# Where in the queues the transfers stand that form sums of the output weights in DRAM

## The chip, the cores and the metric

The kernel runs on one core of one Trainium2 chip. The metric is device time in microseconds (us), lower is better. The kernel before was timed three times; the median is 1558.39 us. One further execution was recorded by the hardware profiler, and all rows quoted below are from it.

Engine names are those of the profile: PE is the matrix engine, PEld its weight loads, DVE the vector engine, ACT the scalar engine, POOL the GpSimd engine. SP only issues transfers (DMAs). A "q" behind an engine's name means its instruction queue, which issues DMAs. DMA queue q1 holds what SP issues, q0 what POOL issues, q10 what ACT issues.

## What is computed

One encoder layer on a sequence of 1024 tokens with model width 1024, in float32. Cut to what matters here:

```python
h = rmsnorm(x, g_mix)
z = h @ w_in                    # pooling channels | q | k | v, 8 heads
y_pool = pool_mixer(z[:, :512], ...)
y_attn = diff_attention(q, k, v, ...)          # two softmax maps per head
gates = sigmoid(h @ w_gate + b_gate)           # 2 x 1024 columns
merged = gates[:, :1024] * (y_pool @ w_branch_pool) \
       + gates[:, 1024:] * (y_attn @ w_branch_attn)
x = x + merged @ w_out
x = x + square(relu(rmsnorm(x, g_ffn) @ w_up)) @ w_down
```

The product with `w_out` is made with seven block products in place of eight. For that it needs sums of the 512 x 512 quarters of `w_out`; with the quarters 11, 12, 21, 22, they are T1 = 11 + 12, T3 = 22 + 12, T2 = 22 + 12 + 11 and T4 = 22 + 12 + 11 + 21 (the signs are handled elsewhere).

## The kernel before, in words

Every float32 product runs as three matmuls on halves of the operands. A helper `split` (lines 132 and 133) makes the halves: ACT writes the high one, and DVE or POOL subtracts to get the low one. `mm3` (lines 139 to 141) issues the three matmuls.

**Startup.** SP loads `x` in eight tiles of 128 tokens, the weights of head 0 in four pairs (`rqkv`, each pair two DMAs of 192 KB) and small vectors. PE runs warm-up products with no use (`warm`), then, for each tile of tokens, transposes the normed tile `hn` into `hT` (lines 564 and 289). The early instructions pass through a helper `q` (line 439), which keeps the written order on each engine. The tiles 0 to 3 of `x` come first; the tiles 4 to 7 are loaded by line 437, outside that fixed order.

**Heads.** A loop of token steps `g` (line 932) covers 8 heads of 8 tiles, 64 steps in all. In each step a written order of stages (`ORDER`) takes the projection `z` (stage A), its normalization (stage B, line 273 on POOL in `rsq`, one step later), the transposes of q and k (C), the scores (D) and so on. Stage W, two steps ahead of a head, loads the next head's weights (`load_w`) and has them split with POOL (`split_w`, lines 132 and 133). Between the steps, fill work is dealt out two steps to a unit: columns of the gate product (`gate_cols`, tiles `frgate`, `fwgate`, `g`) and the pooling groups. A gate column is two units; its weights are loaded by `fill_w` (line 314) in two DMAs of 256 KB and split with POOL.

**The order that is written is not the order that runs.** A planner takes each instruction in order of its place in the program as soon as its inputs and its engine are free by the planner's own clock. Work without inputs is thus issued far ahead of the step in which it is written. `tc.issue_after(ins)` adds one rule: what stands in its block, as far as it is on the engine of `ins`, is issued behind `ins` in that engine's queue. It is an order of issue, with no wait for `ins` to finish.

**The sums.** `sum_steps` (line 919) forms T1 to T4 in DRAM. Four plain copies of 1 MB, issued by SP (line 924), write one quarter into each sum. Seven accumulating DMAs of 1 MB, issued by POOL (line 927), add the others; an add waits for the transfer that wrote the same sum before. The generator is advanced from the token loop (lines 954 and 955): at step 12 all four copies, then one add at each of the steps 18, 24, 30, 36, 42, 48 and 54. Nothing else orders them. After the heads, `w_set` (line 1085) loads the sums with the other operands of the output product (tile `ro`); the first such load of a sum is issued at 848.0 us.

**After the heads** come the two branch products, the gating, the output product (seven products on the sums), the second norm, and the two products of the feed-forward part.

Of the kernel before, what the change touches and what calls it, by code (L numbers as in the profile page):

```python
# [12 lines left out]
ALU = mybir.AluOpType  # L13
# [30 lines left out]
N_W1, N_W2 = 9, 16  # L44
POOL_W = (3,)
G_DIST, G_COLS = 3, 2
SUM_FROM, SUM_STEP = 12, 6

O = "B1 C2 H7 D4 R8 E5 F6 W-2 A0"
ORDER = [(w[0], int(w[1:])) for w in O.split()]  # L50
# [14 lines left out]
def encoder_kernel(  # L65
# [21 lines left out]
    nc = tc.nc  # L87
# [42 lines left out]
    def split(hi, lo, src, lo_eng=None):  # L130

        made = nc.scalar.copy(hi, src)  # L132
        (lo_eng or nc.vector).tensor_tensor(lo, src, f(hi), op=ALU.subtract)  # L133
        return made
# [20 lines left out]
    def fw_tile(shape, name, dt=F32R):  # L155
        return fwpool.tile(shape, dt, tag="fw", name=name)
# [4 lines left out]
    def fr_tile(shape, name):  # L161
        return fp.tile(shape, F32, tag="fr", name=name, bufs=N_FR)
# [90 lines left out]
    mhalf = const.tile([P, NT], F32, name="mhalf")  # L253
# [13 lines left out]
    yd = dram.tile([S, D], F32, name="yd")  # L267
    w_sum = [dram.tile([S // 2, D], F32, name=f"w_sum{i}") for i in range(2)]

    def rsq(dst, ss, n, c):  # L270

        nc.vector.tensor_scalar(dst, ss, c, EPS, op0=ALU.mult, op1=ALU.add)  # L272
        nc.gpsimd.tensor_tensor(dst, dst, mhalf[:, :n], op=ALU.pow)  # L273

    def norm_transpose(xt, gb, t, dst, hn, small, banks):

        th, c0 = t // 4, (t % 4) * P
        ss = small.tile([P, 1], F32, tag="ss", name=f"ss{t}", bufs=2)
        rs = small.tile([P, 1], F32, tag="rs", name=f"rs{t}", bufs=2)
        nc.scalar.activation(hn, xt, AF.Square, accum_out=ss)  # L280
        rsq(rs, ss, 1, 1.0 / D)
        for j in range(2):
            js = slice(j * 512, (j + 1) * 512)
            nc.vector.scalar_tensor_tensor(hn[:, js], xt[:, js], rs, gb[:, js], op0=ALU.mult, op1=ALU.mult)
            trp, trtag = banks[j % len(banks)]
            ps = trp.tile([P, 512], F32, tag=trtag, name=f"hps{t}_{j}")
            for i in range(4):
                k = 4 * j + i
                nc.tensor.transpose(ps[:, i * P : (i + 1) * P], hn[:, k * P : (k + 1) * P], identf)
            for i in range(2):  # L290
                kp = 2 * j + i
                src = ps[:, i * 256 : (i + 1) * 256].rearrange("p (a b) -> p a b", a=2)
                h_hi[t] = split(dst[kp, th, 0][:, :, c0 : c0 + P], dst[kp, th, 1][:, :, c0 : c0 + P], src)
# [16 lines left out]
    def fill_w(src, c0, name):  # L310
        ws = []
        for j in range(2):
            rw = fr_tile([P, 4, P], f"fr{name}_{j}")
            nc.sync.dma_start(
                rw, src[j * 512 : (j + 1) * 512, c0 : c0 + P].rearrange("(kk p) c -> p kk c", p=P)
            )
            w = fw_tile([P, 2, 4, P], f"fw{name}_{j}")
            split(w[:, 0], w[:, 1], rw, nc.gpsimd)
            ws.append(w)
        return ws  # L320
# [22 lines left out]
    def pool_group(g):  # L343
        win = WINDOWS[g]
        ws = fill_w(w_in, g * P, f"pool{g}")
        rg = fr_tile([P, P], f"rgrp{g}")
        nc.sync.dma_start(rg, w_pool_grp[g])
# [35 lines left out]
    def gate_cols(c):  # L383
        with first_gates(c) if c < 3 else nullcontext():
            ws = fill_w(w_gate, c * P, f"gate{c}")
        for th in range(2):
            ps = fill_proj(ws, th, f"g{c}_{th}", spare_bank if c >= G_Z else fill_bank)
            fo = fo_tile(f"go{c}_{th}")
            nc.scalar.activation(fo[:, 0:512], ps, AF.Identity, bias=cols[:, c : c + 1])  # L389
            nc.scalar.dma_start(g_dram[c * P : (c + 1) * P, th * 512 : (th + 1) * 512], fo[:, 0:512])  # L390
            yield
# [23 lines left out]
    with ExitStack() as ph:  # L415
# [279 lines left out]
        def stage_prep(h, t):  # L695
            th = t // 4
            V, ggh = KV[h][1], gghs[h]
            z = st[h, t]["z"]
            sq = s1([P, 256], F32, f"sq{h}_{t}", "sq")
            ms = sp.tile([P, 4], F32, tag="ms", name=f"ms{h}_{t}", bufs=3)  # L700
            nc.scalar.activation(sq, z[:, 0:256], AF.Square)
            nc.vector.tensor_reduce(ms, sq.rearrange("p (a b) -> p a b", a=4), axis=AX.X, op=ALU.add)
            rsq(ms, ms, 4, 1.0 / HD)
            split(V[th][:, t % 4, 0, :], V[th][:, t % 4, 1, :], z[:, 256:384])
            qn = s1([P, 4, HD], F32, f"qn{h}_{t}", "qn", N_QN)
            nc.vector.tensor_tensor(
                qn,
                z[:, 0:256].rearrange("p (a b) -> p a b", a=4),
                ms.unsqueeze(2).broadcast_to([P, 4, HD]),
                op=ALU.mult,  # L710
            )
            nc.gpsimd.tensor_tensor(
                qn[:, 2:4, :], qn[:, 2:4, :], ggh.unsqueeze(1).broadcast_to([P, 2, HD]), op=ALU.mult
            )
            st[h, t] = {"qn": qn}
            yield
# [202 lines left out]
        def sum_steps():  # L919

            q = {f"{i + 1}{j + 1}": w_out[i * 512 : (i + 1) * 512, j * 512 : (j + 1) * 512] for i in range(2) for j in range(2)}
            s = {f"T{i}": w_sum[n][:, c : c + 512] for i, n, c in ((1, 0, 0), (3, 0, 512), (2, 1, 512), (4, 1, 0))}
            for dst, src in (("T1", "11"), ("T3", "22"), ("T2", "22"), ("T4", "22")):
                nc.sync.dma_start(s[dst], q[src])
            yield
            for dst, src in (("T1", "12"), ("T3", "12"), ("T2", "12"), ("T4", "12"), ("T2", "11"), ("T4", "11"), ("T4", "21")):
                nc.gpsimd.dma_start(s[dst], q[src], accum_op=ALU.add)
                yield

        units, made = fillers(), 0  # L930
        sums = sum_steps()
        for g in range(-2, N + 10):
            for t in range(4, NT):
# [186 lines left out]
    def norm_scale(t, src):  # L1120

        ss = squares.pop(t)
        rs = const.tile([P, 1], F32, tag="nrs", name=f"nrs{t}", bufs=2)
        yn = y[t]
        nc.vector.tensor_scalar(rs, ss[:, 0:1], ss[:, 1:2], 1.0 / D, op0=ALU.add, op1=ALU.mult)
        rsq(rs, rs, 1, 1.0)
        for j in range(2):
            js = slice(j * 512, (j + 1) * 512)
            if t < 4:
                nc.vector.scalar_tensor_tensor(yn[:, js], src[j], rs, gfb[:, js], op0=ALU.mult, op1=ALU.mult)  # L1130
            else:
                scaled[t] = nc.vector.tensor_scalar(yn[:, js], src[j], rs, None, op0=ALU.mult)
# [488 lines left out]
```

## Time and profile before

| What | us |
|---|---|
| median of three runs | 1558.39 |
| the three runs | 1558.51, 1558.39, 1557.36 |
| the profiled execution, its own time | 1557.51 |
| span in its trace, first to last instruction | 1555.7 |
| PE busy in the span | 1527.8 |
| DVE, ACT, POOL busy in the span | 1015.3, 794.8, 371.5 |

The span is 1.8 us shorter than the execution's own time, which has a start and an end around it. PE is busy in 98% of the span, but this share counts matmuls at full and at half clock alike. The profile's slices therefore have to be read with the row of the granted clock (PEclk, in tenths) beside the row of PE. A "DMA share" near 1 means that the 16 DMA engines were busy all the time; the GB/s beside it say how much they moved in that time, and the two need not go together.

### The profile page before, as it was taken

The page shows a single profiled execution, that of the slowest core. Times are in us where ns is not written, and L with a number is a line of the kernel's source. Part 1 is how long each engine was busy: PE and PEld are TensorE (multiplying, and loading weights), DVE is VectorE, ACT ScalarE, POOL GpSimd, SP SyncE. Part 2 cuts the span into 40 slices and gives each one's busy share as a digit, 9 for nine tenths or more (in the row PEclk, how much of TensorE's full clock was granted, in tenths as well). Part 3 has the DMA queues.
Part 4 walks back from the last instruction along what each step waited for, and adds up shares of the span by engine and source line. Part 5 has one row for each costly group of instructions (what it writes and reads, how often), then busy time and mean ns, then how long its engine had stood idle before and what let it go on. Part 6 is the DMA issues. An engine that isn't in the chain of part 4 may idle for free.

```text
span 1555.7 us, 21699 instructions
## 1 busy us (share of the span) xinstructions
PE 1527.8 (98%) x7637; PEld 1325.1 (85%) x7637; DVE 1015.3 (65%) x2135; ACT 794.8 (51%) x1653; POOL 371.5 (24%) x457
## 2 busy tenths in 40 slices
PE   7799999999999999999999999999999999999999
PEld 6699999999999999988888887888888878888887
DVE  4477766777677777753444799776665578646662
ACT  4365655555655555554642458565555544333331
POOL 2452515243435343313355530000000000000000
PEclk8799999999999999999999999999999999999999
DMA  9951212111212121326642832546442789637650
GB/s 253 206 125 35 76 36 78 36 55 39 72 40 72 39 76 48 109 78 226 198 158 95 280 146 95 183 154 195 152 143 108 250 313 362 224 122 251 228 191 27
DMA packets 172087, 216.89 MB, mean 139 GB/s; under 512 B 10085, under 2 KB 104010, under 8 KB 171978
## 3 DMA queue, kind: packets, MB, share of 16 engines
q1 hardware_dynamic: 150858, 180.86, 35.3%
q10 hardware_dynamic: 17424, 27.31, 4.8%
q0 software_dynamic: 3696, 7.34, 2.8%
q8 instruction: 60, 0.98, 0.3%
q14 instruction: 49, 0.40, 0.1%
HBM read 161.96 MB, written 65.04 MB: 146 GB/s over the span
## 4 chain that ended last, share of the span: by engine, by line
PE 89%; DMA 5%; DVE 4%; POOL 1%; issue 1%; ACT 1%; POOLq 0%; SPq 0%; ACTq 0%; DVEq 0%
PE z L139 5%; PE z L140 5%; PE z L141 5%; PE Da L140 4%; PE Da L141 4%; PE Da L139 4%; PE g L141 4%; PE g L140 4%; PE g L139 4%; PE Db L139 3%; PE Db L140 3%; PE Db L141 3%; PE X L139 3%; PE X L141 3%; PE X L140 3%; PE sc L769 2%
## 5 line engine op out<-in xcount | busy, mean ns | idle before, releaser
L139 PE MATMUL z<-wqkv,hT 128*128 128x384 f32 x512 | 177.8, 347 | 9.1 <-ACT hT L132 5.8
L141 PE MATMUL z<-wqkv,hT 128*128 128x384 f32 x512 | 176.6, 345 | 0.1
L140 PE MATMUL z<-wqkv,hT 128*128 128x384 f32 x512 | 176.0, 344 | 0.0
L780 ACT ACTIVATE s<-s,nm 128x256 f32<-128x256 f32 (+7 forms) x128 | 99.6, 778 | 78.4 <-DVE nm L772 75.6
L273 POOL TENSOR_TENSOR ms<-ms,mhalf 128x4 f32<-128x4 f32 x64 | 67.4, 1052 | 198.5 <-DVE ms L272 189.1
L139 PEld LDWEIGHTS z<-wqkv,hT 128*128 128x128 f32 x512 | 98.6, 192 | 13.2 <-ACT hT L132 6.8
L139 PE MATMUL g<-hT,fwgate 128*128 128x512 f32 x256 | 100.8, 394 | 0.0
L141 PE MATMUL g<-hT,fwgate 128*128 128x512 f32 x256 | 100.4, 393 | 0.0
L140 PEld LDWEIGHTS z<-wqkv,hT 128*128 128x128 f32 x512 | 98.6, 193 | 2.1 <-DVE wqkv L439 0.3
L140 PE MATMUL g<-hT,fwgate 128*128 128x512 f32 x256 | 100.4, 392 | 0.0
L141 PEld LDWEIGHTS z<-wqkv,hT 128*128 128x128 f32 x512 | 98.3, 192 | 2.0 <-DVE hT L437 0.6
L772 DVE CUSTOM_DVE_ANT_0 s<-sc,dist 128x512 f32<-128x512 f32 (+3 forms) x128 | 74.3, 585 | 20.6 <-PE sc L770 19.7
L769 PE MATMUL sc<-K,Q 128*128 128x512 f32 (+2 forms) x192 | 67.2, 356 | 0.4 <-DVE nm L772 0.4
L770 PE MATMUL sc<-K,Q 128*128 128x512 f32 (+2 forms) x192 | 66.1, 349 | 0.0
L133 DVE TENSOR_TENSOR AS<-s,AS 128x512 fp32r<-128x512 f32 x64 | 43.4, 687 | 33.1 <-ACT AS L132 33.0
L133 POOL TENSOR_TENSOR wqkv<-rqkv,wqkv 128x384 fp32r<-128x384 f32 x56 | 58.8, 1066 | 15.3 <-ACT wqkv L132 12.2
L133 POOL TENSOR_TENSOR fwgate<-frgate,fwgate 128x512 fp32r<-128x512 f32 x32 | 42.4, 1326 | 64.7 <-ACT fwgate L132 62.1
L141 PEld LDWEIGHTS g<-hT,fwgate 128*128 128x128 f32 x256 | 48.1, 188 | 9.5
L139 PEld LDWEIGHTS g<-hT,fwgate 128*128 128x128 f32 x256 | 48.1, 188 | 9.0 <-ACT go L389 0.2
L140 PEld LDWEIGHTS g<-hT,fwgate 128*128 128x128 f32 x256 | 48.1, 188 | 8.8
L133 DVE TENSOR_TENSOR AT_0l<-ta,AT_0h 128x512 fp32r<-128x512 f32 (+1 forms) x48 | 31.9, 665 | 29.4 <-ACT AT_0h L132 29.3
L140 PE MATMUL ba<-yT,wba 128*128 128x512 f32 x128 | 49.8, 389 | 0.0
(483 smaller groups left out, 4603.8 us busy)
## 6 DMA issues: line engine op xcount, KB each, us to landing
wd<-in_w_down_dram SPq DMA_DIRECT2D x56, 512.0 KB, 5.1
wu<-in_w_up_dram SPq DMA_DIRECT2D x32, 512.0 KB, 4.4
udS<-us SPq DMA_DIRECT2D x64, 256.0 KB, 3.0
ur<-udS SPq DMA_DIRECT2D x32, 512.0 KB, 4.8
rqkv<-in_w_in_dram SPq DMA_DIRECT2D x64, 192.0 KB, 2.6
ur<-ud SPq DMA_DIRECT2D x24, 512.0 KB, 5.3
frgate<-in_w_gate_dram SPq DMA_DIRECT2D x32, 256.0 KB, 2.9
g_dram<-go ACTq DMA_DIRECT2D x32, 256.0 KB, 2.1
```

What stands on the lines that cost most here:

```text
L133: (lo_eng or nc.vector).tensor_tensor(lo, src, f(hi), op=ALU.subtract)
L139: nc.tensor.matmul(ps, lhs_hi, rhs_hi, start=first, stop=False, **kw)
L140: nc.tensor.matmul(ps, lhs_hi, rhs_lo, start=False, stop=False, **kw)
L141: return nc.tensor.matmul(ps, lhs_lo, rhs_hi, start=False, stop=last, **kw)
L273: nc.gpsimd.tensor_tensor(dst, dst, mhalf[:, :n], op=ALU.pow)
L769: nc.tensor.matmul(dst, Q[:, i, 0, :], rhs, start=True, stop=False)
L770: nc.tensor.matmul(dst, Q[:, i, 1, :], rhs, start=False, stop=True)
L772: nc.vector.tensor_tensor_reduce(out=s[i][:, c : c + w], in0=sc[:, 0:w], in1=dist[:, o0 + c : o0 + c + w], scale=2.0 ** -(h + 1), scalar=B ...
L780: nc.scalar.activation(s[i][:, 0:n], s[i][:, 0:n], AF.Exp, bias=last, scale=-1.0, accum_out=Z[:, i, t : t + 1])
```

## The change

The transfers of `sum_steps` get a place in their engines' queues, and are dealt out one at a time. Two marks are kept: the last `rsq` instruction on POOL, and the last weight load of the fill work on SP. Each copy is queued behind the latest such load on SP, each add behind the latest `rsq` on POOL. The generator now stops after each copy, and is advanced at every step from 10 on whose number is a multiple of four: the copies at 12, 16, 20 and 24, the adds at 28, 32, 36, 40, 44, 48 and 52. What is moved and added is the same.

```diff
-SUM_FROM, SUM_STEP = 12, 6
+SUM_FROM, SUM_STEP = 10, 4
...
+    marks = {}
+
     def rsq(dst, ss, n, c):
 
         nc.vector.tensor_scalar(dst, ss, c, EPS, op0=ALU.mult, op1=ALU.add)
-        nc.gpsimd.tensor_tensor(dst, dst, mhalf[:, :n], op=ALU.pow)
+        marks["POOL"] = nc.gpsimd.tensor_tensor(dst, dst, mhalf[:, :n], op=ALU.pow).ins
...
-            nc.sync.dma_start(
+            marks["SP"] = nc.sync.dma_start(
                 rw, src[j * 512 : (j + 1) * 512, c0 : c0 + P].rearrange("(kk p) c -> p kk c", p=P)
-            )
+            ).ins
...
             for dst, src in (("T1", "11"), ("T3", "22"), ("T2", "22"), ("T4", "22")):
-                nc.sync.dma_start(s[dst], q[src])
-            yield
+                with tc.issue_after(marks["SP"]):
+                    nc.sync.dma_start(s[dst], q[src])
+                yield
             for dst, src in (("T1", "12"), ("T3", "12"), ("T2", "12"), ("T4", "12"), ("T2", "11"), ("T4", "11"), ("T4", "21")):
-                nc.gpsimd.dma_start(s[dst], q[src], accum_op=ALU.add)
+                with tc.issue_after(marks["POOL"]):
+                    nc.gpsimd.dma_start(s[dst], q[src], accum_op=ALU.add)
                 yield
```

## The prediction

> **What bounds the kernel now.** I read the page's slices first, to find where the matrix engine is not at its peak.
>
> ```profile
> span 1555.7 us, 21699 instructions
> PE   7799999999999999999999999999999999999999
> ...
> PEclk8799999999999999999999999999999999999999
> DMA  9951212111212121326642832546442789637650
> GB/s 253 206 125 35 76 36 78 36 55 39 72 40 72 39 76 48 109 78 226 198 158 95 280 146 95 183 154 195 152 143 108 250 313 362 224 122 251 228 191 27
> ```
>
> Each slice is 38.9 us. The first two show PE idle, the clock below full and the DMA engines full. After that PE is at nine tenths or more to the end. So I cut the first two slices into stages, with the heads as a measure of an undisturbed PE.
>
> ```profile
> core 0: us, PE busy (x) PEld busy (x) DVE busy (x) ACT busy (x) POOL busy (x), PEclk, DMA share, GB/s
> 0.00:10.00 10.00, 6.12 (x36) 5.67 (x36) 0.17 (x1) 1.56 (x2) 2.15 (x26) 1.00 0.76 238
> ...
> 50.00:60.00 10.00, 5.13 (x22) 4.08 (x22) 6.14 (x15) 5.45 (x11) 3.96 (x6) 0.66 1.12 219
> 60.00:70.00 10.00, 4.92 (x15) 3.82 (x16) 3.30 (x10) 3.62 (x9) 3.62 (x4) 0.63 0.56 111
> ...
> 13.20:80.00 66.80, 52.87 (x242) 46.15 (x243) 34.23 (x92) 29.54 (x76) 25.86 (x31) 0.78 0.95 226
> 100.00:600.00 500.00, 500.00 (x2921) 464.29 (x2920) 359.32 (x1093) 287.30 (x742) 195.96 (x268) 1.00 0.18 55
> ```
>
> In the heads, from 100 to 600 us, PE makes 2921 matmuls in 500 us, 0.171 us each, with no idle time. From 13.2 to 80 us it makes 242, worth 242 x 0.171 = 41.4 us, in 66.8 us. So 25.4 us are lost there, part as idle time, part at half clock. The three idle times of PE that matter, and the useless warm-up before them:
>
> ```profile
> 4.15 1.21 PE L439 MATMUL gb<-identf,g_cols 128*128 128x128 f32 x8
> 5.12 2.15 PE L439 MATMUL warm<-ones 128*128 128x256 f32 x16
> 13.23 1.97 PE L439 MATMUL hps<-identf,hn 128*128 128x128 f32 x8 [5.97 <-ACT hn L439]
> ...
> 22.00 0.69 PE L139 MATMUL z<-wqkv,hT 128*128 128x384 f32 x1 [2.76 <-ACT wqkv L439]
> ...
> 64.66 0.69 PE L139 MATMUL z<-wqkv,hT 128*128 128x384 f32 x1 [5.41 <-ACT hT L132]
> ```
>
> Each is traced to a load through the ACT instruction that it waits for:
>
> ```profile
> 9.72 0.63 ACT L439 ACTIVATE hn<-x 128x512 f32<-128x512 f32 x1 [7.08 <-DMA x<-in_x_dram]
> ...
> 21.43 0.51 ACT L439 CAST wqkv<-rqkv 128x384 fp32r<-128x384 f32 x1 [4.29 <-DMA rqkv<-in_w_in_dram]
> ...
> 47.72 1.06 ACT L280 ACTIVATE hn<-x 128x1024 f32<-128x1024 f32 x1 [5.88 <-DMA x<-in_x_dram]
> ...
> 63.72 0.62 ACT L132 CAST fwgate<-frgate 128x512 fp32r<-128x512 f32 x1 [5.17 <-DMA frgate<-in_w_gate_dram]
> ```
>
> The sums are written for steps 12 to 54, but the queues show them in just this stretch, the first copy ahead of everything:
>
> ```profile
> 0.75 0.62 SPq L924 DMA_DIRECT2D w_sum<-in_w_out_dram  x1
> 1.42 1.07 SPq L439 DMA_DIRECT2D x<-in_x_dram  x2
> ...
> 9.71 2.20 SPq L439 DMA_DIRECT2D rqkv<-in_w_in_dram  x4
> ...
> 28.60 2.55 SPq L924 DMA_DIRECT2D w_sum<-in_w_out_dram  x2
> 31.19 5.34 SPq L437 DMA_DIRECT2D x<-in_x_dram  x4
> 40.42 50.79 SPq L314 DMA_DIRECT2D frgate<-in_w_gate_dram  x6
> ```
>
> ```profile
> 9.42 1.29 POOL L927 DMA_DIRECT2D w_sum<-in_w_out_dram  x1 [7.27 <-DMA w_sum<-in_w_out_dram]
> ```
>
> ```profile
> L927 POOL DMA_DIRECT2D w_sum<-in_w_out_dram x7: 1007/1091/1414, 9.4 to 86.7; - x7
> L924 SPq DMA_DIRECT2D w_sum<-in_w_out_dram x4: 507/728/1670, 0.7 to 29.5; - x4
> ...
>   POOL w_sum L927: 19.5, 4
> ...
> DMA to landing us min/median/max: 3.6/12.4/21.3
> ```
>
> All eleven transfers are issued between 0.7 and 86.7 us, 11 MB of what the full DMA engines carry. The weights of head 0 show the effect: the last four of their DMAs go out between 9.71 and 11.91 us, the first add just ahead of them at 9.42 us, and ACT waits for one until 21.43 us. What such loads take by their median over the program:
>
> ```profile
> rqkv<-in_w_in_dram SPq DMA_DIRECT2D x64, 192.0 KB, 2.6
> ...
> frgate<-in_w_gate_dram SPq DMA_DIRECT2D x32, 256.0 KB, 2.9
> ```
>
> **What goes: the first wait.** The first copy leaves the head of SP's queue, so `x` is issued at 0.75 us. By the nearest row, 256 KB in 2.9 us, its first half is there at 3.7 us and the second half, one issue later, by about 4.5. It now starts ACT at 9.72, and from there to the transposes at 13.23 the chain takes 3.5 us. That would give 7.2 to 8.0. Two things hold it back: the gain `gb` ends at 5.36 and must be copied between, and the warm-ups end at 7.27. I take 8.0 us, a gain of 5.2. The bounds are 2.3, if `x` takes twice the row's 2.9 us, and 6.0, when the warm-ups end.
>
> **What goes: the rest of the startup.** With no copy ahead and no add beside them, I let loads land as the medians say. From the transposes on, what is late next is ACT and DVE, which make the operands. I count three remainders of the 25.4 us. Token 0: the casts still come one by one on ACT, 0.5 us each by the row at 21.43, with ACT's other work between them, and PE at full clock needs 3 x 0.17 = 0.5 us for each; I leave 2 us. The three tiles after it have a chain each (norm, transposes, split) that PE cannot run ahead of; another 2 us, an estimate between nothing and the idle time of one such chain. For the tiles 4 to 7, DVE sets the pace:
>
> ```profile
> 50.00:100.00 50.00, 39.87 (x200) 35.50 (x201) 29.66 (x86) 25.91 (x71) 21.85 (x28) 0.83 0.84 163
> ```
>
> DVE is busy 29.66 us here, and PE has 200 x 0.171 = 34.2 us worth of matmuls. In the heads DVE runs at 359 of 500 us, 72%, with no gap in PE. At 72% it would need 41 us, a loss of 7; at a share of 87% none. I take 4. That leaves 8 us of the 25.4 and a gain of 17.3. The bounds are a remainder of 4, and of 15 if the idle time of PE from 50 to 70 us, 20 less 5.13 and 4.92, some 10 us, stays whole beside 5 of the rest.
>
> **What is added in the heads.** Nothing is computed more. POOL issues seven adds there, 1.09 us each by the row of L927, so 7.6 us of POOL's queue. What they wait for has landed: transfers of one sum lie at least four steps apart, and a step is 9.2 us, from one `ms` to the next:
>
> ```profile
> 402.15 1.01 POOL L273 TENSOR_TENSOR ms<-ms,mhalf 128x4 f32<-128x4 f32 x1 [2.38 <-DVE ms L272]
> ...
> 411.34 1.01 POOL L273 TENSOR_TENSOR ms<-ms,mhalf 128x4 f32<-128x4 f32 x1
> 413.06 1.99 POOL L133 TENSOR_TENSOR wqkv<-rqkv,wqkv 128x384 fp32r<-128x384 f32 x2 [0.71 <-ACT wqkv L132]
> ```
>
> Four steps are 37 us against at most 21.3 to land. So the 19.5 us that POOL stood waiting before its adds are gone. Behind each add stand the scaling of k (L712) and, near a head's start, the weight splits. The splits that end at 415.05 are used here:
>
> ```profile
> 413.32 0.52 ACT L132 CAST wqkv<-rqkv 128x384 fp32r<-128x384 f32 x1 [0.34 <-DMA rqkv<-in_w_in_dram]
> ```
>
> ```profile
> 417.68 0.33 PE L139 MATMUL z<-wqkv,hT 128*128 128x384 f32 x1
> ```
>
> That is a slack of 2.6 us, more than 1.09. The adds are hidden by PE's 100% of other work, and cost 0 to 7.6 us if that cover fails. SP's four copies stand behind the loads of gate columns 1 to 4; they are 1 MB each, and what stands behind a copy in q1 waits. The copy at the front delayed `x` from about 4 to 9.7 us, so 5 to 6 us for one collision. Gate loads have tens of us of slack, the weights of head 1 do not, so I bound it by one collision, 5 us. For all of this I take 1 us; the bounds are 0 (nothing here can gain, as PE has no gap in the heads) and 12.6.
>
> One page of the Trainium skill speaks against the move: "SBUF — State Buffer", in its section "SBUF: two separate sides", says that POOL writes the descriptors of its DMAs itself and is locked out while DVE runs certain modes, so that a DMA of about 620 ns took about 3100. By that, the seven adds could cost 7 x 2.5 = 17 us of POOL's time, and the sum, if all of it reached PE, would be 17 us higher. The trace speaks against it here: with DVE busy 59% of the time from 50 to 100 us, no add took over 1.41 us.
>
> **The sum.** 5.2 + 17.3 - 1.0 = 21.5 us. The profiled execution took 1557.5 us, span and 1.8 us around it, so 1536.0. The median of the runs is 0.9 us higher and within their spread, so I keep 1536.
>
> **The rivals.** (1) Half the gain. `issue_after` is an order, not a wait, and gate loads run ahead of their steps: the row at 40.42 shows six of them issued by 91.2 us, so the copies behind columns 1 to 3 can still go out in the startup, beside the tiles 4 to 7 and the weights of head 1. Then the change does only in part what it says, and the 10 us of idle time from 50 to 70 stay: 1536 + 10 = 1546. For it: the copies are bound to loads that the planner sends early. Against it: the adds, the first of which stood beside the latest of the loads, are bound to POOL's work of token 27 and later, which cannot run ahead.
>
> (2) Slower: the adds starve the heads' loads. A load beside the first add took from 11.91 us at the latest to 21.43, 9.5 us in place of 2.6, so 6.9 more; with 2.6 us of slack PE stops for 4.3. Three of the seven adds, at steps 32, 40 and 48, fall at a head's start, where the loads are tight: 13 us, and still faster. The five that make up the gain only bring the time back; it decides from the sixth on, and with all seven it is 1536 + 30 = 1566. Against it: half of a head's weights are loaded long ahead, and the DMA share in the heads is 0.18. "DMA: Bandwidth & Descriptors" of the skill, in its section on queues, rings and completion order, says that each DMA engine takes turns between queues by packets, which would make a load beside an add slow anywhere; the load of 9.5 us agrees.
>
> (3) No change: the startup's loads alone fill the DMA engines, and `x` lands as late without the copies. Then the waits stay, near 1557.5. Against it: 1 MB of the 2.4 MB moved in the first 10 us (238 GB/s) is the copy, and the adds stand at the very waits.
>
> (4) The cover in the heads fails: POOL's order of work is so tight at the adds that each reaches PE whole, at the longest time of the row of L927, 7 x 1.41 = 9.9 us in place of the 1 us that I counted: 1536 + 9 = 1545. For it: slacks of 2.6 us at a head's start. Against it: POOL is busy 196 us of 500 in the heads, 39%.
>
> **How the numbers follow.** I give my forecast 0.77, the half gain 0.13, the failed cover 0.04, no change 0.03, the starved heads 0.03. A change of 0.2%, 3.1 us, is about what a measurement of this kernel can tell from none. Forecast, half gain and failed cover are faster, 0.94; same 0.03, slower 0.03. The range goes from 1529 (gains of 6.0 and 21.4 and no cost: 27.4, and 1 us for the spread) to 1548, the half gain and the spread of the runs. It leaves out (2) and (3), 0.06, and the ends of the forecast's own bounds.
>
> **What would show it.** Right: no line L924 or L927 before the gate column 1 load; the first `hps` near 8 us; no idle time of PE above 3 us after it; the granted clock full from there; the tiles 4 to 7 no longer waited for at L280; the adds at some 250 to 560 us, about 1.1 us each, and `ro` loads unchanged. Wrong: PE idle in the heads before `z`, ACT waits for `rqkv` above 2 us at steps 32, 40 and 48, or `x` still landing near 9.7 us. Then the loads or the heads, and not the sums' place, set the end.

## The result, and the profile after

The changed kernel takes 1533.55 us, the median of four runs (1532.62 to 1535.27). The kernel before took 1558.27 us in the four runs beside it (1557.36 to 1558.51). The ratio is 0.9844, with a 95% interval of 0.9827 to 0.9861. The profiled execution took 1532.97 us, 24.5 us less than the one before (1557.51).

In this kernel all lines behind the start of the diff are two to four numbers higher: the helper of the early instructions is L441, the gate and channel weights are loaded at L316, the copies stand at L927 and the adds at L931. The slices of its page:

```profile
span 1531.2 us, 21704 instructions
...
PE   9999999999999999999999999999999999999999
...
PEclk9999999999999999999999999999999999999999
DMA  7322011332424221327544633555433899537750
GB/s 241 120 73 73 30 59 47 73 85 58 107 61 107 58 90 49 112 97 259 177 140 162 211 150 116 173 184 167 152 124 110 289 317 373 189 124 261 228 191 28
```

The first two slices now look like the rest. PE is at nine tenths and its clock is full. The DMA engines have gone from 9 and 9 tenths there to 7 and 3. What left them shows up in slices 8 to 14, which read 1112121 before and 3324242 now. The stages, as they were cut before (each engine's busy time, then PEclk, DMA share and GB/s):

```profile
0.00:10.00 10.00, 8.83 (x52) 8.08 (x52) 4.84 (x11) 6.01 (x12) 2.75 (x27) 1.00 0.78 240
...
50.00:60.00 10.00, 10.00 (x58) 9.26 (x57) 7.57 (x24) 7.29 (x22) 3.61 (x7) 1.00 0.14 46
60.00:70.00 10.00, 10.00 (x59) 9.44 (x58) 7.48 (x20) 5.35 (x17) 6.76 (x8) 1.00 0.56 177
...
7.39:80.00 72.61, 70.48 (x408) 63.41 (x406) 60.10 (x154) 46.70 (x128) 37.79 (x47) 1.00 0.55 177
100.00:600.00 500.00, 497.47 (x2897) 461.17 (x2896) 360.79 (x1076) 281.99 (x729) 199.77 (x271) 1.00 0.28 71
```

Two rows carry the account. From its first useful work to 80 us, PE makes 408 matmuls, worth 408 x 0.171 = 69.8 us, in 72.6 us: 2.8 us are lost where 25.4 were. From 100 to 600 us it makes 2897 matmuls where it made 2921: 24 x 0.171 = 4.1 us are lost that were not before. The rows of the waits of before, in the timeline of the changed kernel, and the row that starts useful work:

```profile
3.47 0.63 ACT L441 ACTIVATE hn<-x 128x512 f32<-128x512 f32 x1 [0.80 <-DMA x<-in_x_dram]
...
7.39 1.10 PE L441 MATMUL hps<-identf,hn 128*128 128x128 f32 x8
...
10.10 0.51 ACT L441 CAST wqkv<-rqkv 128x384 fp32r<-128x384 f32 x1 [0.54 <-DMA rqkv<-in_w_in_dram]
...
16.62 2.12 SPq L439 DMA_DIRECT2D x<-in_x_dram  x4
18.50 1.06 ACT L282 ACTIVATE hn<-x 128x1024 f32<-128x1024 f32 x1
...
27.59 2.07 SPq L316 DMA_DIRECT2D frgate<-in_w_gate_dram  x2
29.71 0.61 SPq L927 DMA_DIRECT2D w_sum<-in_w_out_dram  x1
```

`x` is used at 3.47 us in place of 9.72, and `hps` begins at 7.39 in place of 13.23: 5.8 us. The last wait for head 0's weights is 0.54 us long, where it was 4.29. The tiles 4 to 7 are issued at 16.62 in place of 31.19 and their first one is used without a wait at 18.50. The first copy leaves at 29.71, behind the loads of gate column 1. So 5.8 + (25.4 - 2.8) - 4.1 = 24.3 us, of 24.5 measured. The sums' lines (min, median and max in ns, first and last start):

```profile
L927 SPq DMA_DIRECT2D w_sum<-in_w_out_dram x4: 505/510/607, 29.7 to 109.2; - x4
...
L931 POOL DMA_DIRECT2D w_sum<-in_w_out_dram x7: 1088/1137/1275, 265.0 to 502.1; - x7
its engine sat idle before it (us, times) until:
who waited for it (us, times):
...
DMA to landing us min/median/max: 8.6/11.5/12.5
```

POOL no longer stands before an add; there were 19.5 us of that. An add lands in 11.5 us (median), where the seven adds of before took 16.5 (the 12.4 quoted ahead is the median of the adds, the copies and the loads of the sums together). The new loss is one place, and the longest wait of PE from 100 to 700 us names it:

```profile
PE po L139 <- ACT AT_0h L132: 2.5, 1, 2.5
...
```

```profile
265.04 1.27 POOL L931 DMA_DIRECT2D w_sum<-in_w_out_dram  x1
268.09 0.34 SPq L349 DMA_DIRECT2D rgrp<-in_w_pool_grp_dram  x1
277.27 0.30 ACT L132 CAST wgrp<-rgrp 128x128 fp32r<-128x128 f32 x1 [6.24 <-DMA rgrp<-in_w_pool_grp_dram]
...
277.87 0.56 ACT L132 CAST AT_0h<-ta 128x512 fp32r<-128x512 f32 x1
...
278.49 0.58 PE L139 MATMUL po<-AT_0h,V 128*128 128x256 f32 x1 [2.53 <-ACT AT_0h L132]
```

The first add leaves at 265.04 us. Three us later SP loads `rgrp`, the 64 KB of pooling group 0. They are used 9.2 us after their issue. ACT takes its work in order, so the cast of `wgrp`, whose first product begins only at 342.7 us, holds up what stands behind it, `AT_0h` among it: ACT stands for 6.24 us, and PE runs dry for 2.53. Behind that stop the granted clock is below full as well:

```profile
277.30:290.00 12.70, 11.51 (x61) 10.63 (x62) 8.46 (x27) 7.01 (x23) 3.24 (x6) 0.87 0.11 34
```

A clock of 0.87 over 12.7 us is worth some 1.6 us. With the 2.5 us of the stop that makes the 4.1 us lost in the heads.

### The profile page after: what moved, and what is told of

Read it like the earlier page. It is cut to its first block, busy times and chain, and to the rows that moved or that the text cites. A ratio compares the mean times of both kernels' runs of the same rounds, so it can differ in the third digit from the quotient of the medians.

```text
span 1531.2 us, 21704 instructions
## 1 busy us (share of the span) xinstructions
PE 1518.8 (99%) x7637; PEld 1317.0 (86%) x7637; DVE 1024.6 (67%) x2135; ACT 792.8 (52%) x1653; POOL 372.6 (24%) x457
## 3 DMA queue, kind: packets, MB, share of 16 engines
q1 hardware_dynamic: 150858, 180.86, 35.9%
q0 software_dynamic: 3696, 7.34, 3.1%
## 4 chain that ended last, share of the span: by engine, by line
PE 95%; DVE 2%; DMA 1%; ACT 1%; issue 0%; SPq 0%; POOL 0%; POOLq 0%; ACTq 0%; DVEq 0%
PE z L139 5%; PE z L141 5%; PE z L140 5%; PE Da L140 4%; PE Da L141 4%; PE Da L139 4%; PE g L139 4%; PE g L140 4%; PE g L141 4%; PE Db L140 3%; PE Db L139 3%; PE Db L141 3%; PE X L139 3%; PE X L140 3%; PE X L141 3%; PE sc L771 2%
## 5 line engine op out<-in xcount | busy, mean ns | idle before, releaser
L139 PE MATMUL z<-wqkv,hT 128*128 128x384 f32 x512 | 174.1, 341 | 1.7 <-ACT hT L132 1.1
L141 PE MATMUL z<-wqkv,hT 128*128 128x384 f32 x512 | 173.8, 340 | 0.2 <-DVE hT L439 0.2
L140 PE MATMUL z<-wqkv,hT 128*128 128x384 f32 x512 | 173.4, 339 | 0.0
L139 PEld LDWEIGHTS z<-wqkv,hT 128*128 128x128 f32 x512 | 96.5, 189 | 4.6 <-ACT hT L132 1.2
L141 PEld LDWEIGHTS z<-wqkv,hT 128*128 128x128 f32 x512 | 96.4, 188 | 2.5 <-DVE hT L441 0.7
L140 PEld LDWEIGHTS z<-wqkv,hT 128*128 128x128 f32 x512 | 96.4, 188 | 2.4 <-DVE wqkv L441 0.3
L774 DVE CUSTOM_DVE_ANT_0 s<-sc,dist 128x512 f32<-128x512 f32 (+3 forms) x128 | 74.1, 585 | 20.3 <-PE sc L772 19.4
L133 POOL TENSOR_TENSOR wqkv<-rqkv,wqkv 128x384 fp32r<-128x384 f32 x56 | 59.3, 1095 | 12.5 <-ACT wqkv L132 11.0
L714 POOL TENSOR_TENSOR qn<-qn,ggh 128x128 f32<-128x128 f32 x64 | 37.1, 579 | 53.3 <-DVE qn L708 44.1
```

What stands on the lines that cost most here:

```text
L139: nc.tensor.matmul(ps, lhs_hi, rhs_hi, start=first, stop=False, **kw)
L140: nc.tensor.matmul(ps, lhs_hi, rhs_lo, start=False, stop=False, **kw)
L141: return nc.tensor.matmul(ps, lhs_lo, rhs_hi, start=False, stop=last, **kw)
L714: nc.gpsimd.tensor_tensor(qn[:, 2:4, :], qn[:, 2:4, :], ggh.unsqueeze(1).broadcast_to([P, 2, HD]), op=ALU.mult)
L774: nc.vector.tensor_tensor_reduce(out=s[i][:, c : c + w], in0=sc[:, 0:w], in1=dist[:, o0 + c : o0 + c + w], scale=2.0 ** -(h + 1), scalar=B ...
```

## The experiments

The theory after the result has three parts. The startup's gain is two gains, one for each kind of transfer, and each comes from loads without slack (`x`, head 0's weights, the tiles 4 to 7). In the heads an add costs nothing by itself; it costs where a load without slack lies beside it. And an add that has to wait for another in POOL's queue does cost. The rivals: the steps do it alone, without the marks; adds in the heads cost wherever they stand; POOL's waits are hidden by its slack.

**Only the adds moved.** The copies lose their mark.

```diff
-                with tc.issue_after(marks["SP"]):
-                    nc.sync.dma_start(s[dst], q[src])
+                nc.sync.dma_start(s[dst], q[src])
```

> The four copies are no longer queued behind the gate loads, the adds stay behind POOL's work of the heads. My theory: the copy at the front of SP's queue costs the first wait, and the other copies delay the tiles 4 to 7, while the adds cost the load of the last weights of head 0 and the late gate loads. So the first transposes of hn come back to about 13 us (+5.8 us), the wait of 4.3 us for rqkv at 21 us stays away, and the time is 1533.5 + 5.8 + about 4 for the tiles 4 to 7 = 1543 (1539 to 1547). Rival (the adds alone did the harm, the copies are hidden by the warm-up): at most 1536. Rival (the copies did nearly all of it): 1553 or more.

Measured: 1546.96 us (1543.26 to 1548.26), ratio 0.9925 (0.991 to 0.994). Its timeline, and its windows in the two stretches:

```profile
0.75 0.62 SPq L926 DMA_DIRECT2D w_sum<-in_w_out_dram  x1
...
13.15 1.94 PE L441 MATMUL hps<-identf,hn 128*128 128x128 f32 x8 [4.97 <-ACT hn L441]
...
23.02 2.78 SPq L926 DMA_DIRECT2D w_sum<-in_w_out_dram  x2
...
38.07 1.06 ACT L282 ACTIVATE hn<-x 128x1024 f32<-128x1024 f32 x1 [5.66 <-DMA x<-in_x_dram]
```

```profile
13.15:80.00 66.85, 62.29 (x336) 55.95 (x337) 46.29 (x129) 38.95 (x107) 28.34 (x35) 0.95 0.47 155
...
100.00:600.00 500.00, 496.84 (x2883) 461.11 (x2882) 359.20 (x1079) 282.08 (x730) 197.18 (x270) 0.99 0.27 68
```

The first wait is back, whole, and so is the wait for the tiles 4 to 7, behind the other three copies. From 13.15 to 80 us PE does 336 x 0.171 = 57.5 us of work, a loss of 9.4 us. So moving the adds gave 25.4 - 9.4 = 16.0 us of the startup. Moving the copies gave 5.8 + 9.4 - 2.8 = 12.4. In the heads 2921 - 2883 = 38 matmuls are missing, 6.5 us, and the profiled execution's gain of 9.3 us (1557.51 - 1548.26) is about what 16.0 - 6.5 leaves. The one long wait of PE in the heads is the same stop at `rgrp`: issued at 279.81 us, 2.6 us behind the first add, it is used at 289.67, and PE idles 3.16 us.

**Only the copies moved.** The adds lose their mark.

```diff
-                with tc.issue_after(marks["POOL"]):
-                    nc.gpsimd.dma_start(s[dst], q[src], accum_op=ALU.add)
+                nc.gpsimd.dma_start(s[dst], q[src], accum_op=ALU.add)
```

> The seven adds are no longer queued behind POOL's work of the heads, the copies stay behind the gate loads. An add can go out as soon as its copy has landed, so the first at some 35 to 40 us, the others between 45 and 130 us. My theory: by then x and the weights of head 0 are in, so only gate loads and the weights of head 1 stand beside the adds; the first transposes stay at 7.4 us, the loss from 275 to 280 us goes (-4.1), and PE loses 2 to 8 us before 130 us: 1531 to 1538. Rival (adds beside any load of the startup stop PE as they did before): 1545 or more. Rival (POOL waits for a copy's landing with its queue blocked, and PE with it): POOL waits of 10 us and more in front of L931 and PE idle behind them.

Measured: 1541.42 us (1538.91 to 1544.86), ratio 0.99 (0.9884 to 0.9917), slower than expected. An unmarked add goes out as soon as the transfers before it allow, and the copies had become late; so the seven adds stand between 38.8 and 143.8 us. The four up to 78.2 us cost little: from 7.39 to 80 us PE makes 405 matmuls, 3 fewer than in the changed kernel. But then adds of one sum come close together. The timeline of POOL, and of DVE and PE behind it (start, duration; in brackets the idle time before and what ended it):

```profile
134.91 1.10 POOL L930 DMA_DIRECT2D w_sum<-in_w_out_dram  x1 [7.67 <-DMA w_sum<-in_w_out_dram]
135.64 0.87 POOL L714 TENSOR_TENSOR qn<-qn,ggh 128x128 f32<-128x128 f32 x1
...
143.82 1.03 POOL L930 DMA_DIRECT2D w_sum<-in_w_out_dram  x1 [7.02 <-DMA w_sum<-in_w_out_dram]
144.48 1.44 POOL L275 TENSOR_TENSOR ms<-ms,mhalf 128x4 f32<-128x4 f32 x1
...
145.95 0.42 DVE L708 TENSOR_TENSOR qn<-z,ms 128x256 f32<-128x256 f32 x1 [6.43 <-POOL ms L275]
...
149.36 0.80 PE L771 MATMUL sc<-K,Q 128*128 128x512 f32 x1 [5.62 <-DVE nm L774]
```

POOL stands at the add, with the scaling and the norm of the next tokens (`qn`, `ms`) behind it; DVE then waits for `ms`, and PE idles 5.62 us. The expectation had named this as the rival, with waits of 10 us and more; they are 7 to 8 us long. The test of it alone is below.

This run also corrects the account of the startup. The two gains worked out above, 16.0 us for the adds and 12.4 for the copies, hold only in that order. An add waits for its copy, so when the copies move, the adds follow them out of the way without a mark: 405 matmuls in the startup are all but the whole gain. Moving the copies is enough there; the marks on the adds pay later, where they keep adds of one sum apart.

**Only the steps.** Both marks are left out; the steps from 10, every four, and the pause behind each copy stay.

> Only the numbers of the steps and the stop after each copy are kept, no transfer is queued behind anything. My theory: the place in the program orders nothing for work without inputs, so the transfers go out in the startup as before, the first copy at 0.75 us, and the time is that of before, 1558 (1555 to 1561). Rival (the wider spread of the copies over the steps is what helps): below 1550.

Measured: 1558.1 us (1557.11 to 1559.74), ratio 1.0 (0.9991 to 1.001). The first copy is at 0.75 us again, and the adds begin at 8.8 us and end at 87.1. The steps without the order of issue do nothing. The other half, the marks with the old steps, was not run.

**The steps from 14.** All eleven transfers stand one slot later, and the first add goes out at 305 us, no longer beside `rgrp`.

```diff
-SUM_FROM, SUM_STEP = 10, 4
+SUM_FROM, SUM_STEP = 14, 4
```

> As the changed kernel, one round of four steps later: copies at steps 16 to 28, adds at 32 to 56. My theory: the only loss that the change brought is one load of 64 KB (rgrp, pooling group 0) that went out at 268 us beside the first add and took 9 us, with ACT waiting 6.2 us for it. With the first add at some 305 us that load is alone: ACT does not wait at 270 us, PE has no idle time there, and the time is 1533.5 - 4.1 = 1529.5 (1528.5 to 1531). Rival (POOL's issue of an add, or any add in the heads, costs PE the time): the loss moves to the next add, and the time stays 1533 to 1534.

Measured: 1529.53 us (1529.21 to 1531.58), ratio 0.982 (0.9805 to 0.9834). Its timeline at the place of the loss, and its window of the heads:

```profile
267.53 0.34 SPq L349 DMA_DIRECT2D rgrp<-in_w_pool_grp_dram  x1
269.29 0.30 ACT L132 CAST wgrp<-rgrp 128x128 fp32r<-128x128 f32 x1 [0.38 <-DMA rgrp<-in_w_pool_grp_dram]
```

```profile
100.00:600.00 500.00, 500.00 (x2922) 463.42 (x2921) 364.20 (x1089) 284.70 (x736) 201.12 (x273) 1.00 0.29 74
```

The same load is used 1.8 us after its issue in place of 9.2, and PE has its 2922 matmuls in the 500 us, as before the change, though the same seven adds run in them.

**The load moved, not the adds.** This is the other way to part the two: the adds stay at the steps of the changed kernel, and `rgrp` is loaded ahead of the group's channel weights.

```diff
-        ws = fill_w(w_in, g * P, f"pool{g}")
         rg = fr_tile([P, P], f"rgrp{g}")
         nc.sync.dma_start(rg, w_pool_grp[g])
...
         split(wg[:, 0, :], wg[:, 1, :], rg, nc.gpsimd)
+        ws = fill_w(w_in, g * P, f"pool{g}")
```

> The changed kernel's steps (from 10, every four) and marks, with one thing moved: the pooling group's own weights (rgrp, 64 KB) are loaded and split ahead of the group's channel weights, no longer behind them, so the load of group 0 should not fall beside the first add at 265 us. Theory: the 4 us that the changed kernel loses to the kernel with steps from 14 are this one load's, so it gains them back: 1529 to 1531, and no ACT wait for rgrp above 1 us near 277 us. Rival: the first add's early place costs by itself (POOL's queue, or other loads beside it), and the time stays at 1533 to 1534 with the load moved.

Measured: 1531.25 us (1530.7 to 1532.89), ratio 0.9829 (0.9815 to 0.9844). That is 0.25 us above the upper end of what I expected. With the first add still at 265.8 us, the stop near 277 us is gone, so the add's early place costs nothing by itself. But from 100 to 600 us PE makes 2910 matmuls, 11 short of before, which is 1.9 us. Its timeline shows one place of the same kind:

```profile
425.11 1.14 POOL L931 DMA_DIRECT2D w_sum<-in_w_out_dram  x1
...
429.98 0.37 SPq L316 DMA_DIRECT2D frpool<-in_w_in_dram  x1
...
436.63 0.62 ACT L132 CAST fwpool<-frpool 128x512 fp32r<-128x512 f32 x1 [4.07 <-DMA frpool<-in_w_in_dram]
```

With `rgrp` out of its way, a load of the channel weights falls beside the fifth add. It is used 6.6 us after its issue, and ACT stands for 4.07.

**The three side by side.** The changed kernel, the steps from 14 and the moved load differ by 2 to 4 us, so they were timed once more, side by side.

> The changed kernel once more, beside the two variants of it on the same chip, since the times to be told apart differ by 2 to 4 us. If the pooling group's load beside the first add is what it still loses, it stands 3 to 4 us above the kernel with steps from 14: 1532.5 to 1535. If the differences between the earlier runs were between chips, all three fall within 1 us of each other.

> The kernel with steps from 14 once more, on the same chip as the changed kernel: 1529 to 1531.5, 3 to 4 us below it.

> The changed kernel's steps with the pooling group's weights loaded first, once more on the same chip. In its trace PE loses 4.0 us less than the changed kernel from 250 to 300 us and 1.1 us more from 435 to 440 us, where a load of the group's channel weights now lies beside an add. So 2.5 to 3.5 us below the changed kernel: 1530 to 1532.

Measured: 1533.2 us (1532.5 to 1534.13) for the changed kernel, 1529.71 (1528.89 to 1530.09) from 14, and 1531.08 (1530.32 to 1532.88) with the load moved, beside 1558.34 before; ratios 0.9839 (0.9825 to 0.9853), 0.9815 (0.9801 to 0.9829) and 0.9826 (0.9813 to 0.984). The differences hold, and the version with steps from 14 is faster than both kernels. The moved load is 2.1 us below the changed kernel, a little less than the 2.5 to 3.5 that I expected.

**The sums left out.** The kernel makes no transfer of the sums, and the output product reads as many blocks of `w_out` in their place (a second change to the code, not shown here), so it computes another output.

```diff
-                next(sums, None)
+                pass
...
```

> The eleven transfers of the sums are left out, and the output product reads quarters of w_out where it read the sums, so its output is not the reference's; the loads of the output product keep their number and size. This is the floor: what the eleven transfers still cost anywhere. Theory: with the steps counted from 14, the transfers cost next to nothing (PE loses 0.6 us from 200 to 300 us there, and the startup is without a wait for them), so the floor is at most 1 us below that kernel's 1529.5: 1528 to 1530. Rival: the copies still lengthen the startup (PE loses some 10 us in the first 100 us of the changed kernel, and the copies at 29.7, 37.4 and 61.5 us lie in it); then the floor is 3 to 6 us below, 1523 to 1526.

Measured: 1530.26 us (1529.56 to 1531.26), ratio 0.9822 (0.9807 to 0.9836), 0.26 us above the upper end of what I expected. That is no less than with the steps from 14. So eleven transfers of 1 MB, well placed, cost nothing that can be measured, and the copies still lying in the startup cost nothing either: without them PE makes 412 matmuls from 7.39 to 80 us, with them (steps from 14) 411.

**The adds packed densely.** Seven adds in seven steps, right behind one another.

```diff
-            if g >= SUM_FROM and g % SUM_STEP == 0:
+            if (g in (16, 20, 24, 28) or 32 <= g < 39):
```

> The copies stay behind gate columns' loads (steps 16, 20, 24 and 28), the seven adds follow at the steps 32 to 38, one per token step of 9.2 us, while an add takes about 10 us to land. So for some 65 us an add is nearly always on its way, and every load of the heads that falls in there lies beside one. Two adds of the same sum are two or more steps apart, so none should wait for another for long. Theory: what an add costs depends on whether a load with little slack falls beside it (the pooling group's load cost 4.1 us in the changed kernel), so I expect one or two such stops, 1532 to 1542. If loads with slack are all that fall in there, 1529 to 1531. The second rival of the prediction (each add beside a head's start costs 4.3 us): one head starts in these steps (step 32), so 1533 to 1535 by that alone.

Measured: 1529.73 us (1529.47 to 1529.93), ratio 0.9818 (0.9803 to 0.9833). I expected one or two stops; there is none. Its line of adds and its window around them:

```profile
L931 POOL DMA_DIRECT2D w_sum<-in_w_out_dram x7: 1082/1102/1277, 306.0 to 363.0; - x7
```

```profile
305.00:375.00 70.00, 70.00 (x415) 65.06 (x414) 53.42 (x157) 36.96 (x97) 31.18 (x41) 1.00 0.81 146
```

The DMA share is 0.81 for 70 us, and PE makes 415 matmuls, as many as the kernel with steps from 14 in the same stretch at a share of 0.33. So an add beside the heads' loads is not a cost in general. `rgrp` and the channel weights fell in there too (at 353.7 and from 326.9 us), where nothing waited for them.

**Adds that wait for one another.** The kernel with steps from 14, with the adds of one sum put together: T1 at step 32, T3 at 36, two of T2 at 40, three of T4 at 44. As many bytes, at places with room.

```diff
-            for dst, src in (("T1", "12"), ("T3", "12"), ("T2", "12"), ("T4", "12"), ("T2", "11"), ("T4", "11"), ("T4", "21")):
+            for k, (dst, src) in enumerate((("T1", "12"), ("T3", "12"), ("T2", "12"), ("T2", "11"), ("T4", "12"), ("T4", "11"), ("T4", "21"))):
...
-                yield
+                if k not in (2, 4, 5):
+                    yield
```

> Steps from 14, every four, the marks kept, but the adds are paired so that later adds of one sum stand close behind the earlier one in POOL's queue: T1 at step 32, T3 at 36, two of T2 at 40, three of T4 at 44. An add waits in the queue until the one before it on the same sum has landed, about 10 us after its issue. No more bytes are moved than in the kernel with steps from 14 (1529.5 us). Theory: what cost 8 us with the adds unmarked was POOL standing at such a wait with the scaling of q and k behind it. Here three adds wait, up to 6 to 9 us each, PE loses several us for each: 1538 to 1550. Rival: POOL's wait is hidden by its slack (it is busy 39% in the heads) and only loads beside an add cost: 1529 to 1532.

Measured: 1540.23 us (1539.28 to 1540.36), ratio 0.9884 (0.9867 to 0.99); 10.7 us above the kernel that it is made from. The waits of POOL, and its timeline at the last of them:

```profile
POOL w_sum L931 <- DMA w_sum<-in_w_out_dram: 20.3, 3, 7.1
```

```profile
438.17 1.03 POOL L931 DMA_DIRECT2D w_sum<-in_w_out_dram  x1 [7.08 <-DMA w_sum<-in_w_out_dram]
...
447.60 1.01 POOL L931 DMA_DIRECT2D w_sum<-in_w_out_dram  x1 [6.94 <-DMA w_sum<-in_w_out_dram]
448.27 1.41 POOL L275 TENSOR_TENSOR ms<-ms,mhalf 128x4 f32<-128x4 f32 x1
...
449.71 0.43 DVE L708 TENSOR_TENSOR qn<-z,ms 128x256 f32<-128x256 f32 x1 [12.86 <-POOL ms L275]
...
453.18 0.69 PE L771 MATMUL sc<-K,Q 128*128 128x384 f32 x1 [7.10 <-DVE Q L742]
```

Three waits, 20.3 us of POOL. Behind the last of them the norm `ms` comes late, DVE has waited 12.86 us for it, and PE 7.10 for the product made from it. The first wait (before the add at 394.88 us) costs PE nothing: it makes 282 matmuls from 380 to 430 us with 49.98 us busy. The other two come in a row: from 430 to 460 us PE makes 121 matmuls, 20.7 us of work in 30, and 9.3 of the 10.7 us are lost there, 7.25 of them as idle time and the rest at a granted clock of 0.83. The product at 453.18 us begins 7.10 us after PE ran out of work, at 446.08. Without the 6.94 us of the last wait the same chain would have had it ready at about 446.2 (an estimate). So POOL's slack covered one such wait here, and not two in a row.

## Why the prediction was right

The forecast was 1536.0 us. The time is 2.4 us under it, and the terms were these (25.4 less the remainder of 8 is 17.4; I had written 17.3):

| Term | Predicted | Measured |
|---|---|---|
| first wait | 5.2 | 5.8 |
| loss left in the startup after it | 8 | 2.8 |
| cost in the heads | 1.0 | 4.1 |
| sum | 21.5 | 24.3 |

The two sizes that I missed go opposite ways: 5.2 us too little gained in the rest of the startup, 3.1 us too little lost in the heads. That the forecast came so close is in part luck.

**The first wait** went as worked out. ACT starts on `x` at 3.47 us, by the median of a 256 KB load; the chain behind it takes 3.9 us. The experiment with free copies brings the wait back whole, so it is the copy's alone.

**The rest of the startup** had the right mechanism and a remainder that was too large. I left 2 us for token 0's casts, 2 for the chains of the next three tiles and 4 for DVE. From 7.39 to 14 us PE waits once, 0.5 us. From 14 us, to 100, its one wait of over 0.2 us is this, with the row of ACT that it waits for:

```profile
39.49 0.93 ACT L132 CAST hT<-hps 128x256 fp32r<-128x256 f32 x3 [2.05 <-DVE hT L133]
...
40.01 0.41 PE L139 MATMUL z<-wqkv,hT 128*128 128x384 f32 x1 [1.09 <-ACT hT L132]
```

All three remainders were too large. The step that failed most in size is the one on DVE: I held its share in the heads, 72%, for the pace that it could keep. From 7.39 to 80 us it is busy 60.10 of 72.61 us, 83%. It does hold PE up once, through ACT: from 36 to 40 us it is busy 3.96 of 4.00, and PE's 1.09 us stand behind it. So the mechanism of that term is there, at about 1 us in place of 4. A share that an engine has where another engine is the bound is what it is asked for, not what it can do. One row is missing from the three idle times that the prediction lists: at 55.37 us PE had stood 3.46 us, longer than the 2.76 at 22.00, behind the late tiles 4 to 7. It is inside the 25.4 us all the same, and it went with the rest.

**The heads** cost four times my 1.0, inside the bound of 12.6. The step that failed is the choice of the loads: I looked at the weights of the heads and at the gate columns, and not at the pooling group's. What I priced for the weights of a head, a stop of some 4 us where a load with little slack lies beside an add, happened once, at `rgrp`. That POOL's own time for the adds is hidden was right: 7 x 1.14 us are there, and dense adds cost nothing. That no add waits was right too, and it is what the four steps between them are worth: the last experiment lost 10.7 us without them. The rule of "SBUF — State Buffer" in the Trainium skill ("SBUF: two separate sides"), by which a DMA issued by POOL took about 3100 ns beside DVE work that locked POOL out, did not show here: at most 1275 ns, with DVE busy 360.79 of 500 us. Whether DVE ran the modes of that rule beside the adds is not shown.

**The rivals.** Half the gain: its condition came true and its harm did not. Three copies go out at 29.7, 37.4 and 61.5 us, behind gate loads that run early, as it said. But by then the tiles 4 to 7 have left SP's queue. The starved heads: true at one load of many. The turn-taking between queues of which "DMA: Bandwidth & Descriptors" of the Trainium skill speaks fits the load of 9.2 us; the dense adds show that the time need not suffer from it. No change: its condition was false, `x` is used at 3.47 us once the copy is gone. The failed cover is what adds in the wrong order give, by waits and not by their issue time.

**The signs** named ahead: no copy or add before gate column 1's load, `hps` near 8 us (7.39), no idle time of PE above 3 us (2.53), no wait at L282 for the tiles 4 to 7, adds of 1.1 us, `ro` loads as before (3.7 us to land), all came. The full clock came but for the stretch behind the stop at `rgrp` (0.87 from 277.3 to 290 us). The adds stand at 265 to 502 us, near the 250 to 560. Of the signs for wrong, one came under another name: an ACT wait of over 2 us, for `rgrp` and not for `rqkv`.

## What to carry to other kernels

A big transfer without a due time costs by what it stands beside: ask which small load next to it has no slack, and which in-order engine takes that load's first use. The DMA share answers neither: 0.81 cost nothing in one place, and one 1 MB add beside a 64 KB load cost 4 us in another. A transfer that must wait for another belongs so far behind it, in the queue of the engine that issues it, that the wait is over when its turn comes.

## What the runs showed of the hardware

I had not expected a load to be slowed that much while the DMA engines were not full. Beside a single add, `rgrp` took 9.2 us in place of 1.8. The two queues of the changed kernel over its whole span (packets, MB, the time that the packets took as a share of 16 engines' span), and its window from the end of the add's issue to the use of `rgrp`:

```profile
q1 hardware_dynamic: 150858, 180.86, 35.9%
...
q0 software_dynamic: 3696, 7.34, 3.1%
```

```profile
266.30:277.20 10.90, 9.66 (x62) 9.14 (x60) 4.00 (x12) 2.48 (x7) 3.39 (x4) 1.00 0.88 148
```

The 7.34 MB of q0 are the seven adds. In 3.1% of 1531.2 us, 47 us, that is about 155 GB/s while their packets run; for what SP issues (q1) it is 180.86 MB in 550 us, 329 GB/s. In the window beside the add the share is 0.88 and 148 GB/s are moved. So an add keeps the engines busy while less is counted as moved. And the small load is not served at its own pace: issued 3 us behind the add, it is used at 277.27 us, 12.2 us after the add's issue, and that add landed after 12.5. The same holds in two other runs: with free copies `rgrp` is used 12.5 us after its add's issue (the add landed after 12.8), and with the moved load `frpool` after 11.5 (10.9). Among the dense adds, where nothing waited, the one store of 128 KB (`y_dram`) whose landing the profile shows took 8.0 us, 1.8 in the kernel with steps from 14. How the engines divide their time between the two was not measured by itself.
